# Identity products ahead of the first product, and a later release for the memory tokens' preparation

## The chip, the cores and the metric

The kernel runs on one core of one Trainium2 chip. The metric is the device time of one execution in microseconds (us), as the median of several runs. Engines are named as in the profile: PE is TensorE (matrix products), DVE is VectorE, ACT is ScalarE, POOL is GpSimd, SP is the engine that issues the DMAs.

## The reference

One decoder layer for 1024 tokens of width 1024 in float32: a normalisation, two groups of heads side by side (a gated recurrent one, the mLSTM, and a forgetting attention), a cross-attention into 256 memory tokens, a squared-ReLU MLP and a last normalisation. The part around the change is the start of it:

```python
xn  = rmsnorm(x, ln1)                    # x: 1 x 1024 x 1024
...                                      # w_in (1024 x IN_COLS) gives q, k, v, gates of both groups
b   = jnp.cumsum(fc, axis=-1)            # log forget gates, per head
m_t = jnp.maximum(b + m, jnp.max(dmat, axis=-1))
...
memn = rmsnorm(mem, ln_mem)              # 256 memory tokens, used much later
k, v = jnp.split(memn @ w_kv, 2, axis=-1)
```

## The kernel before

**Products.** A float32 product is made of three products in the chip's rounded format float32r: each operand is cut into a high part (a copy on ACT, L132 or L135) and a low part (a subtraction on DVE, L133 or L136), and `mm3` (L184, L185, L186) adds low times high, high times low and high times high in one PSUM bank. So a weight or an activation can be used only when both engines have cut it.

**The first stage (L372 to L407).** It computes the mLSTM values of the first two heads and the gates, for 8 tiles of 128 tokens, from x with 1024 input channels in 8 steps k. The first half of the tokens has its 4 tiles in the banks `mm`, `tp`, `m2` (printed as `m` in some views) and `tp`: for each k four tiles times three products, 12 products of 128x272. The second half has three tiles in the `sc` banks and, after the stage, the fourth in `mm`. Before a step k its weights (`cut_w`) and its x (`cut_x`) are cut. Sums of squares of x are added into `wide` on DVE (L361), and give the reciprocal root `rcol` (L196, L204 to L206, POOL between). `first_sink(hf, t)` then reads a bank on ACT and DVE, scales by `rcol`, and writes the values (L135, L136) and the gates' column (L370). The block `with in_order()` keeps PE, ACT, DVE and POOL in the written order; the rest of the program is ordered by a scheduler from costs of its own.

**What follows.** `token_major` makes the values of the other two heads, 8 tiles of 24 products (128x256), in the banks `tp`, `m2`, `tp`, `sc`, `mm`, `sc`, `sc` and so on in turn; each tile is read by ACT (L135) and DVE (L136). On the way stand the gates: DVE works out a polynomial of the gates (L427 to L431), PE transposes the result (L446, L451), ACT copies it (L447), DVE scans it twice along the tokens (L452, L456), and PE transposes again (L467). Then come projections with 128x512 products: `conv_silu` (tile `tp`, and a second half in `mm`) and `fx_project` (tile `m2`). Their weights are loaded (L172) into two buffers `wr` and cut by L132 and L133.

**The memory tokens.** `mem_prepare` (L280 to L294) works on `mem` in four chunks of 128x512. A chunk is loaded into a buffer `r_f` (L284; there are two), squared on ACT (L220, `r_c`), added up on DVE (L224, `r_b`, from the second chunk on), cut with the gain in two halves (ACT L135 into `r_p`, DVE L136 in place in `r_f`), and both parts are stored to `hmd` in DRAM (L292). A third load must wait until the first chunk's store has emptied its buffer. `hmd` is read back by one DMA at L1040.

The call stands far down in the code, under a release:

```python
banks[:] = ["mm", "tp", "m2", "tp"]
with tc.issue_after(last_sum.ins):
    mem_prepare()
ready = ml_project(0)
```

`issue_after(ins)` puts the block's instructions that run on the engine of `ins` behind `ins` in that engine's queue. `last_sum` is an addition on DVE, so this holds for the DVE instructions of `mem_prepare` (L224, L136); it is an order and not a wait, and the loads of the first two chunks need none of these instructions.

```python
    square_to(wide[2], 1, 7)
    add_to(wide[1], wide[0])
    last_sum = add_to(wide[1], wide[2])
tiles[1].append(ps_tile("mm")[:, :WV])
for k in range(KT):
    first_values(1, k, (3,))
rsqrt_sums(wide[1], rcol[:, 4:8], 4, 2)
for t in range(4):
    first_sink(1, t)
```

PSUM is dealt out by tag: three `sc` banks, two `tp`, and one each of `mm`, `m2` and `ov`. A tile that takes over a bank waits until its last tile was read.

## Time and profile before

| | us |
|---|---|
| median of 3 runs | 1536.44 |
| the three runs | 1536.03, 1536.44, 1536.86 |
| the profiled execution's own time | 1535.99 |
| its span | 1534.2 |
| PE busy | 1507.5 (98%) |
| DVE busy | 1111.3 (72%) |
| ACT busy | 731.0 (48%) |
| POOL busy | 508.5 (33%) |
| PE idle before its first product | 7.47 |

The span runs from the first to the last instruction that the profile records. A row of the timeline gives start, duration, engine, line, operation, output<-input, shape and count, and in brackets the idle time before it with what ended it. A row of the waits gives who waited for whom, the total, the number of times and the longest. The mean granted clock of PE over the span is 0.998 of full.

### The profile page before, as it was taken

The page shows a single profiled execution, that of the slowest core. Times are in us where ns is not written, and L with a number is a line of the kernel's source. Part 1 is how long each engine was busy: PE and PEld are TensorE (multiplying, and loading weights), DVE is VectorE, ACT ScalarE, POOL GpSimd, SP SyncE. Part 2 cuts the span into 40 slices and gives each one's busy share as a digit, 9 for nine tenths or more (in the row PEclk, how much of TensorE's full clock was granted, in tenths as well). Part 3 has the DMA queues.
Part 4 walks back from the last instruction along what each step waited for, and adds up shares of the span by engine and source line. Part 5 has one row for each costly group of instructions (what it writes and reads, how often), then busy time and mean ns, then how long its engine had stood idle before and what let it go on. Part 6 is the DMA issues. An engine that isn't in the chain of part 4 may idle for free. (4 is left out here: it accounts for less than half of the span.)

```text
span 1534.2 us, 22052 instructions
## 1 busy us (share of the span) xinstructions
PE 1507.5 (98%) x7729; PEld 1262.1 (82%) x7729; DVE 1111.3 (72%) x1716; ACT 731.0 (48%) x1365; POOL 508.5 (33%) x543
## 2 busy tenths in 40 slices
PE   8999999999999999999999999999999999999997
PEld 8878888889898887788888877787787888888887
DVE  7756666764788884854457889898887667887665
ACT  7324343434687773543444457665665621121224
POOL 0002130404355441521110023545455365663322
PEclk9999999999999999999999999999999999999999
DMA  6422233446787958963334528776667777676623
GB/s 215 131 79 76 96 104 112 129 138 161 238 250 217 290 195 280 315 206 125 124 125 164 172 93 299 240 254 240 230 243 273 303 285 283 268 272 237 245 96 110
DMA packets 121531, 303.54 MB, mean 198 GB/s; under 512 B 13502, under 2 KB 28152, under 8 KB 113996
## 3 DMA queue, kind: packets, MB, share of 16 engines
q1 hardware_dynamic: 121420, 302.13, 57.7%
q8 instruction: 61, 1.00, 0.3%
q14 instruction: 50, 0.41, 0.1%
HBM read 202.22 MB, written 99.86 MB: 197 GB/s over the span
## 5 line engine op out<-in xcount | busy, mean ns | idle before, releaser
L184 PE MATMUL tp<-act,wl 128*128 128x512 f32 (+1 forms) x448 | 176.4, 394 | 1.2 <-ACT row L1339 0.7
L185 PE MATMUL tp<-act,wh 128*128 128x512 f32 (+1 forms) x448 | 175.6, 392 | 0.0
L186 PE MATMUL tp<-act,wh 128*128 128x512 f32 (+1 forms) x448 | 175.1, 392 | 0.0
L133 DVE TENSOR_TENSOR wl<-wr,wh 128x1024 fp32r<-128x1024 f32 (+2 forms) x99 | 129.6, 1309 | 25.2 <-ACT wh L132 24.7
L132 ACT ACTIVATE wh<-wr 128x1024 fp32r<-128x1024 f32 (+2 forms) x99 | 99.1, 1001 | 88.8 <-PE tp L186 34.3
L184 PE MATMUL mm<-act,wl 128*128 128x512 f32 (+1 forms) x336 | 130.6, 389 | 1.4 <-DVE r_c L518 0.9
L186 PE MATMUL mm<-act,wh 128*128 128x512 f32 (+1 forms) x336 | 129.2, 384 | 0.0
L185 PE MATMUL mm<-act,wh 128*128 128x512 f32 (+1 forms) x336 | 128.9, 384 | 0.0
L184 PE MATMUL m<-act,wl 128*128 128x512 f32 (+1 forms) x312 | 120.7, 387 | 1.6 <-DVE r_a L916 1.3
L186 PE MATMUL m<-act,wh 128*128 128x512 f32 (+1 forms) x312 | 119.5, 383 | 0.0
L185 PE MATMUL m<-act,wh 128*128 128x512 f32 (+1 forms) x312 | 119.2, 382 | 0.0
L184 PEld LDWEIGHTS tp<-act,wl 128*128 128x128 f32 x448 | 84.3, 188 | 21.0 <-ACT row L1339 1.2
L186 PEld LDWEIGHTS tp<-act,wh 128*128 128x128 f32 x448 | 84.3, 188 | 19.1
L185 PEld LDWEIGHTS tp<-act,wh 128*128 128x128 f32 x448 | 84.4, 188 | 18.7
L184 PE MATMUL sc<-act,wl 128*128 128x512 f32 (+1 forms) x248 | 97.1, 392 | 0.9 <-DVE wl L133 0.8
L185 PE MATMUL sc<-act,wh 128*128 128x512 f32 (+1 forms) x248 | 96.8, 390 | 0.0
L186 PE MATMUL sc<-act,wh 128*128 128x512 f32 (+1 forms) x248 | 96.8, 390 | 0.0
L132 ACT ACTIVATE wh<-z 128x1024 fp32r<-128x1024 f32 (+1 forms) x54 | 55.5, 1028 | 82.6 <-POOL z L1410 59.8
L1410 POOL TENSOR_TENSOR z<-wr 128x256 f32<-128x256 f32 x56 | 50.5, 923 | 131.2 <-DMA wr<-w_ff2q 114.3
L133 DVE TENSOR_TENSOR wl<-z,wh 128x1024 fp32r<-128x1024 f32 (+1 forms) x54 | 74.5, 1380 | 8.1 <-ACT wh L132 7.9
L132 ACT ACTIVATE w<-wr 128x768 fp32r<-128x768 f32 (+2 forms) x31 | 25.5, 823 | 105.0 <-PE tp L184 32.5
L184 PEld LDWEIGHTS mm<-act,wl 128*128 128x128 f32 x336 | 63.4, 189 | 14.3 <-DVE r_c L518 1.2
(685 smaller groups left out, 4286.2 us busy)
## 6 DMA issues: line engine op xcount, KB each, us to landing
act<-right SPq DMA_DIRECT2D x49, 1024.0 KB
right<-w SPq DMA_DIRECT2D x56, 256.0 KB
wr<-w_ff2q SPq DMA_DIRECT2D x28, 512.0 KB
right<-r_d SPq DMA_DIRECT2D x49, 256.0 KB
right<-r_e SPq DMA_DIRECT2D x49, 256.0 KB
act<-fqk SPq DMA_DIRECT2D x48, 256.0 KB
wr<-w_in SPq DMA_DIRECT2D x20, 512.0 KB
wr<-w_ff SPq DMA_DIRECT2D x20, 512.0 KB
```

Source lines behind the costliest of these rows:

```text
L132: s.activation(hi, src, AF.Copy)
L133: return v.tensor_tensor(out=lo, in0=src, in1=hi.bitcast(F32), op=ALU.subtract)
L184: nc.tensor.matmul(ps, w[1], x[0], start=first, stop=False, skip_group_check=more)
L185: nc.tensor.matmul(ps, w[0], x[1], start=False, stop=False, skip_group_check=more)
L186: nc.tensor.matmul(ps, w[0], x[0], start=False, stop=last, skip_group_check=more)
L1410: g.tensor_tensor(out=o, in0=x, in1=y, op=op)
```

## The change

Two edits. Right after the constants, 28 matrix products of the 128x128 identity with itself are written into an `ov` bank that nothing reads, so they stand first in PE's queue. And the block of `mem_prepare` is released by the last instruction of the last `first_sink` of the first stage (L370, on DVE) in place of `last_sum` (L361, on DVE).

```diff
     vec = const("vec", [P, a["vec"].shape[1]])
 
+    busy = ov_()
+    for _ in range(28):
+        nc.tensor.matmul(busy[:, :P], ident, ident, start=True, stop=True)
+
     def split(hi, lo, src, scale=None):
...
         mv_sink(4 * hf + t, 0, ps[:, :256])
-        v.tensor_scalar(out=z[:, 4 * hf + t], in0=ps[:, 256:], scalar1=rcol[:, 4 * hf + t : 4 * hf + t + 1], scalar2=None, op0=ALU.mult)
+        return v.tensor_scalar(out=z[:, 4 * hf + t], in0=ps[:, 256:], scalar1=rcol[:, 4 * hf + t : 4 * hf + t + 1], scalar2=None, op0=ALU.mult)
...
         add_to(wide[1], wide[0])
-        last_sum = add_to(wide[1], wide[2])
+        add_to(wide[1], wide[2])
...
     for t in range(4):
-        first_sink(1, t)
+        last_sink = first_sink(1, t)
...
-    with tc.issue_after(last_sum.ins):
+    with tc.issue_after(last_sink.ins):
         mem_prepare()
```

Since the scheduler orders what is outside `in_order()`, the second edit also moves other instructions; all differences lie in the first 100 us. In the changed kernel every line from 129 on has a number 4 higher (L136 is L140, L446 is L450), and buffers count one or some more. The prediction uses the line numbers of before.

On DVE, around the second reciprocal root (`rcol`), before:

```order
L204 TENSOR_TENSOR c_t_37_439<-c_y_36_437 128x4
L205 SCALAR_TENSOR_TENSOR c_t_37_439<-c_t_37_439,c_var_35_435 128x4
L224 TENSOR_TENSOR r_b_64_776<-r_c_71_801,r_b_64_776 128x512
L206 SCALAR_TENSOR_TENSOR rcol_80<-c_t_37_439,c_y_36_437 128x4
L136 SCALAR_TENSOR_TENSOR r_f_70_799<-r_f_70_799,vec_77,r_p_72_804 128x256 x2
L136 SCALAR_TENSOR_TENSOR act_8_94<-m2_48_523,rcol_80,act_8_94 128x2x128
```

and after:

```order
L208 TENSOR_TENSOR c_t_38_468<-c_y_37_466 128x4
L209 SCALAR_TENSOR_TENSOR c_t_38_468<-c_t_38_468,c_var_36_464 128x4
L210 SCALAR_TENSOR_TENSOR rcol_109<-c_t_38_468,c_y_37_466 128x4
L140 SCALAR_TENSOR_TENSOR act_9_123<-m2_49_552,rcol_109,act_9_123 128x2x128
L140 SCALAR_TENSOR_TENSOR act_8_122<-sc_23_158,rcol_109,act_8_122 128x2x128
```

The sum and the cuts of the third chunk (`r_b`, `r_f`) have left this place; the read of the `m2` bank follows `rcol` directly.

On DVE, in the gates' polynomial (`w4`), ahead of the read of the sixth value tile of `token_major` (in the bank `tp_57_665` before, `tp_58_694` after) and the first scan, before:

```order
L430 SCALAR_TENSOR_TENSOR w4_28_135<-w4_28_135 128x96
L136 SCALAR_TENSOR_TENSOR act_8_94<-m2_56_638,rcol_80,act_8_94 128x2x128
L430 SCALAR_TENSOR_TENSOR w4_28_135<-w4_28_135 128x96 x5
L431 SCALAR_TENSOR_TENSOR w4_28_135<-w4_28_135 128x96
L136 SCALAR_TENSOR_TENSOR act_8_94<-tp_57_665,rcol_80,act_8_94 128x2x128
L452 SCALAR_TENSOR_TENSOR act_39_473<-w4_40_474,act_39_473 12x1024
```

and after:

```order
L140 SCALAR_TENSOR_TENSOR act_9_123<-m2_57_667,rcol_109,act_9_123 128x2x128
L434 SCALAR_TENSOR_TENSOR w4_29_164<-w4_29_164 128x96
L228 TENSOR_TENSOR r_b_65_805<-r_c_72_830,r_b_65_805 128x512
L434 SCALAR_TENSOR_TENSOR w4_29_164<-w4_29_164 128x96
L140 SCALAR_TENSOR_TENSOR r_f_71_828<-r_f_71_828,vec_77,r_p_73_833 128x256 x2
L434 SCALAR_TENSOR_TENSOR w4_29_164<-w4_29_164 128x96
L228 TENSOR_TENSOR r_b_65_805<-r_c_75_842,r_b_65_805 128x512
L140 SCALAR_TENSOR_TENSOR r_f_74_840<-r_f_74_840,vec_77,r_p_76_845 128x256
L434 SCALAR_TENSOR_TENSOR w4_29_164<-w4_29_164 128x96
L140 SCALAR_TENSOR_TENSOR r_f_74_840<-r_f_74_840,vec_77,r_p_76_845 128x256
L140 SCALAR_TENSOR_TENSOR act_9_123<-tp_58_694,rcol_109,act_9_123 128x2x128
```

The third and fourth chunk's sums and cuts now stand here, ahead of the read of the `tp` bank.

On PE, around the gates' transposes (from `w4`, L446 and L451), before:

```order
L446 MATMUL mm_52_609<-ident_65,w4_28_135 12x128 x4
L446 MATMUL sc_53_615<-ident_65,w4_28_135 12x128 x4
L451 MATMUL sc_54_621<-ident_65,w4_28_135 4x128 x4
...
L467 MATMUL ov_60_746<-ident_65,act_39_473 128x4 x8
L184 MATMUL tp_90_879<-act_5_91,wl_87_848 128x512
L185 MATMUL tp_90_879<-act_6_92,wh_86_847 128x512
L186 MATMUL tp_90_879<-act_5_91,wh_86_847 128x512
```

and after:

```order
L188 MATMUL tp_91_908<-act_6_120,wl_88_877 128x512
L189 MATMUL tp_91_908<-act_7_121,wh_87_876 128x512
L190 MATMUL tp_91_908<-act_6_120,wh_87_876 128x512
...
L450 MATMUL mm_53_638<-ident_65,w4_29_164 12x128 x4
L450 MATMUL sc_54_644<-ident_65,w4_29_164 12x128 x4
L455 MATMUL sc_55_650<-ident_65,w4_29_164 4x128 x4
...
L471 MATMUL ov_61_775<-ident_65,act_40_502 128x4 x8
L188 MATMUL tp_91_908<-act_6_120,wl_88_877 128x512
```

Seven of the eight groups of three of the `tp` projection (`conv_silu`) now stand ahead of the transposes; one is left behind L471, and the 24 of the `m2` projection (`fx_project`) follow it. The new tile `tp_91_908` takes over the bank of `tp_58_694`.

## The prediction

> **What bounds the kernel now.** I read first the busy line and the chain of the page, then TensorE's waits, then the timeline of the places the change touches.

> ```profile
> PE 1507.5 (98%) x7729; PEld 1262.1 (82%) x7729; DVE 1111.3 (72%) x1716; ACT 731.0 (48%) x1365; POOL 508.5 (33%) x543
> PE 34%; DVE 3%; issue 1%; ACT 1%; DMA 0%; DVEq 0%; POOLq 0%; POOL 0%; ACTq 0%
> ```

> TensorE (PE) is busy 98% of the span, and the chain runs mostly through it. So a microsecond is won only where PE idles or works slowly, and lost wherever PE is made to wait. Of its waits three lie near the edits:

> ```profile
> PE mm L184 <- DVE wl L133: 7.5, 1, 7.5
> PE m L184 <- DVE act L136: 0.8, 1, 0.8
> PE mm L184 <- DVE r_c L518: 0.9, 1, 0.9
> ```

> They are the idle start before the first product, a wait for a bank that VectorE (DVE) has not read, and one at 95 us. All numbers below are microseconds on the clock of the profiled run of before, whose own time is 1535.99.

> **Part 1: the identity products.**

> ```profile
> 1.24 0.29 POOL L118 TENSOR_SCALAR_AFFINE_SELECT ident<-ident 128x128 f32<-128x128 f32 x1
> 7.47 0.57 PE L184 MATMUL mm<-wh,act 128*128 128x272 f32 x1 [7.47 <-DVE wl L133]
> 10.33 0.43 PE L184 MATMUL mm<-wh,act 128*128 128x272 f32 x1
> 12.83 0.29 PE L184 MATMUL mm<-wh,act 128*128 128x272 f32 x1
> 14.31 0.29 PE L184 MATMUL mm<-wh,act 128*128 128x272 f32 x1
> 21.83 0.29 PE L184 MATMUL sc<-wh,act 128*128 128x272 f32 x1
> 14.91 0.75 DVE L136 SCALAR_TENSOR_TENSOR act<-act,vec,act 128x512 fp32r<-128x512 f32 x1
> 1504.61 1.05 PE L211 MATMUL mm<-ident,c_r 128*128 128x128 f32 x8
> ```

> The `mm` rows are the first of the 12 products of each k. The first two groups take 10.33−7.47=2.86 and 12.83−10.33=2.50, the third 14.31−12.83=1.48: early products run at half rate. Full rate would save 12.83−7.47−2×1.50=2.36. The identity is ready at 1.24+0.29=1.53. Eight products of its shape take 1.05, so 0.13 each, at most doubled while slow: 28 take under 28×0.26=7.3 and about 28×0.21=5.9 by the ratio of the slow and fast groups. They end near 7.5, inside TensorE's idle time before 7.47, on an engine that has nothing else to do; nothing waits for the bank they write. At the worst end they finish at 8.8, and then eight fast groups of 1.50 would end at 20.8 instead of the value below.

> How much of the 2.36 arrives? With groups of 1.50 from 7.47 the sixth (k=5) would start at 14.97, but its operand's low part is done only at 14.91+0.75=15.66. From there three groups end at 15.66+3×1.50=20.16, where before the next stage starts at 21.83. The gain is 1.65, with 0.67 of spare time ahead of k=5; the ends are 2.36 (if the cut of k=5 moves up too) and 1.0 (products late as above: 21.83−20.8). Everything up to the last product of this stage and the next follows PE, so I carry the 1.65 on as a shift. [...]

> **Part 2a: the bank wait that goes.**

> ```profile
> 46.26 0.28 PE L186 MATMUL tp<-wh,act 128*128 128x256 f32 x1
> 47.37 0.38 PE L184 MATMUL m<-wh,act 128*128 128x256 f32 x1 [0.83 <-DVE act L136]
> 44.70 0.63 ACT L220 ACTIVATE r_c<-r_f 128x512 f32<-128x512 f32 x1 [1.74 <-DMA r_f<-mem]
> 43.75 0.16 DVE L205 SCALAR_TENSOR_TENSOR c_t<-c_t,c_var 128x4 f32<-128x4 f32 x1
> 45.36 0.69 DVE L224 TENSOR_TENSOR r_b<-r_c,r_b 128x512 f32<-128x512 f32 x1 [1.46 <-ACT r_c L220]
> 45.97 0.15 DVE L206 SCALAR_TENSOR_TENSOR rcol<-c_t,c_y 128x4 f32<-128x4 f32 x1
> 46.05 0.87 DVE L136 SCALAR_TENSOR_TENSOR r_f<-r_f,vec,r_p 128x256 fp32r<-128x256 f32 x2
> 46.84 0.48 DVE L136 SCALAR_TENSOR_TENSOR act<-m,rcol,act 128x256 fp32r<-128x256 f32 x1
> ```

> PE's next slot was 46.38; it started at 47.37: 0.99 lost. DVE's read of the bank (46.84) stood behind L224, which waited for a memory load. In the changed order L206 follows L205 directly (43.75+0.20−1.65=42.3), and the read is done by 43.1, against a slot at 46.38−1.65=44.73. Gain 0.99. PE is then 1.65+0.99=2.64 ahead.

> **Part 2b: the tp bank.** The memory pieces now stand later on DVE, two of them (the third and fourth chunk, each one load, one square, two cuts and two stores) among the L430s, ahead of the read of the sixth token tile's tp bank. PE in turn has 21 of the 24 products of the next projection (tp, 128x512) ahead of the gate transposes L446, and their first needs that bank.

> ```profile
> 49.22 0.23 DVE L370 TENSOR_SCALAR w<-mm,rcol 128x16 f32<-128x16 f32 x1
> 54.00 0.25 DVE L430 SCALAR_TENSOR_TENSOR w<-w 128x96 f32<-128x96 f32 x1
> 54.16 0.48 DVE L136 SCALAR_TENSOR_TENSOR act<-m,rcol,act 128x256 fp32r<-128x256 f32 x1
> 38.25 1.72 SPq L292 DMA_DIRECT2D hmd<-r_f  x2
> 40.68 0.33 SPq L284 DMA_DIRECT2D r_f<-mem  x1
> 53.82 0.25 ACT L248 ACTIVATE row<-ov 8x128 f32<-8x128 f32 x1
> 56.50 0.60 PE L446 MATMUL mm<-ident,w 128*12 128x128 f32 x4
> 45.24 0.89 ACT L135 ACTIVATE r_p<-r_f,vec 128x256 fp32r<-128x256 f32 x2
> 56.70 0.47 ACT L135 ACTIVATE act<-tp,rcol 128x256 fp32r<-128x256 f32 x1 [2.64 <-PE tp L186]
> 387.76 0.46 SPq L1040 DMA_DIRECT2D act<-hmd  x1
> 57.21 0.48 DVE L136 SCALAR_TENSOR_TENSOR act<-tp,rcol,act 128x256 fp32r<-128x256 f32 x1 [0.94 <-ACT act L135]
> ```

> PE is free for them where L446 stood: 56.50−2.64=53.86. If the third memory load is there in time, ScalarE (ACT) squares it (L220) behind the L248 copy: 53.82+0.25−2.64=51.4, plus 0.63 is 52.0. From there DVE has two L224 (45.97−45.36=0.6 each), four L136 of r_f (46.84−46.05=0.8 for two) and three L430 (54.16−54.00=0.16 each), 3.3 in all, then the read of the bank, 0.48: 55.7. PE loses 55.7−53.86=1.8.

> If the load is late: the last first_sink (L370) ends 49.22+0.23−46.84=2.6 after the read that ends part 2a begins, 45.2. Chunk 0's cut, the first memory work behind it, takes 0.88; its store to hmd goes out at about 46.15, the next load 2.43 after it (38.25 to 40.68), at 48.6. A load took up to 44.70−40.68=4.02: 52.6, L220 to 53.25, and 3.8 later 57.05, a loss of 3.2. The fourth load waits for chunk 1, which DVE leaves 0.6+0.8 after chunk 0, at 47.5; by the same steps it lands by 54.1, is squared by 54.7, and with one L224, two cuts, one L430 and the read behind it (2.0) gives 56.8 at most, inside these ends. ACT's part of this read (56.70) stands behind the same chunks' squares and two cuts each (0.89) there, so it ends at 54.7+0.89+0.47=56.1 at the latest, and DVE's part, which must follow it, at 56.6: also inside. On SP the third weight load now goes ahead of the first store and the row's two transfers ahead of the last four stores; the memory is read back only at 387.76, so I cost this at nothing, and POOL's order is unchanged. Without memory work in the way the bound is 57.21+0.48−56.50=1.2. I take the middle of 1.8 and 3.2: **2.5**.

> **Part 2c: the gate chain.** The transposes L446 start a chain over ACT and DVE, two scans (L452, L456), behind which DVE cuts the weights (L133 at 65.53) of the projection that follows (`m`, 128x512).

> ```profile
> 58.23 2.28 DVE L452 TENSOR_TENSOR_SCAN act<-w,act 12x1024 f32<-12x1024 f32 x1 [0.54 <-ACT act L447]
> 65.53 1.20 DVE L133 TENSOR_TENSOR wl<-wr,wh 128x1024 fp32r<-128x1024 f32 x1
> 64.15 0.50 PE L184 MATMUL tp<-act,wl 128*128 128x512 f32 x1
> 69.85 0.39 PE L184 MATMUL m<-act,wl 128*128 128x512 f32 x1
> ```

> From L446 to those weights: 65.53+1.20−56.50=10.2. Before, PE filled this with 64.15−56.50=7.65 of products and 24 of the projection in 69.85−64.15=5.70, so it came to `m` at 69.85, 3.1 after they were ready at 66.73. Now 21 of the 24 are spent ahead of L446; three remain, 0.71, and 7.65+0.71=8.36. PE waits 10.23−8.36=**1.87**. The order is fixed on both engines; the bounds are 0 (the chain speeds up by as much) and 2.6 (its scans wait once more).

> **Sum.** −1.65−0.99+2.5+1.87=+1.7; with 1.8 to 3.2 for part 2b, +1.0 to +2.4. The wait at 95 us (L518, 0.9) keeps its length, since both sides move together. Own time 1535.99+1.7=1537.7; the median of the runs is 1536.44, 0.45 above the profiled run: **1538.1**, with 1537.4 to 1538.9 as the case's own range. This is under 0.2% (3.07 us), about what a measurement of this kernel can tell from no change; so faster is under 1533.4 and slower over 1539.5.

> **Rivals.**

> *A. The new waits don't come.* DVE may find both memory chunks loaded and pass them while PE is still in the sc products, and the weights may be cut ahead of the second scan. Then −2.64: 1533.8, or 1532.9 if the L518 wait goes too. For it: L224 had only one wait of this kind in before (1.46). Against it: DVE is one queue, the read stands behind all of these pieces in it, and 3.3 of them are plain work that no early load removes; and the gate chain is 10.2 long whatever the loads do. If only one comes, −2.64+1.87 or −2.64+2.5: 1535.7 to 1536.3.

> *B. The identity products raise no clock.* Then 1.65 is missing: 1539.8. No row shows the clock after identity products alone. [...]

> *C. The new waits cost the clock as well: slower.* The kernel's end shows what a stall can do:

> ```profile
> 1527.30 0.71 PE L211 MATMUL mm<-ident,c_r 128*128 128x128 f32 x4 [1.62 <-DVE c_r L1552]
> 1525.00:1530.00 5.00, 1.39 (x10) 1.11 (x10) 2.54 (x9) 0.33 (x1) 0.71 (x1) 0.80 0.26 88
> ```

> (The second row is a window: its length, the busy times of PE, weight load, DVE, ACT and POOL, then granted clock, DMA share and GB/s.) In 1525 to 1530 PE is busy 1.39 of 5 and the mean granted clock 0.80, so about 2 of the 5 at half. A wait of 1.62 stands in it. The wait of part 2b (up to 3.2) could bring the same, and the restart cost 2.36 at the kernel's start: 1538.1+2.4=1540.5. [...] Against it: the 7.65 and 5.70 of dense work around it.

> **How the numbers follow.** The forecast 55% (1537.4 to 1538.9), one wait only 14% (1535.7 to 1536.3), A 9% (1533.8; half of that below 1533.4), B 8% (1539.8, half above 1539.5), C 14% (1540.5). Range 1535.0 to 1540.5: it holds the forecast, the single wait, B and half of C, 84%, and leaves out A and C's upper half, about 16%. Faster: half of A, 0.05. Slower: C and half of B, 0.18. Same: 0.77.

> **What would show it.** Right: the stage after the eight k-groups starts at about 20.2 and the fourth `mm` group is as short as the first; no wait of PE for act L136 at 45; one of 1.8 to 3.2 near 54 ahead of the 128x512 tp products; one near 1.9 for wl ahead of `m`. The part 2b term is wrong if r_f<-mem lands before 51.4 and DVE is through by 54; part 2c is wrong if `m` starts without idle time. Products at half rate behind either wait mean C; a slow first group after the identity products means B.

## The result, and the profile after

The changed kernel took 1546.14 us in the median (1544.14 to 1546.69), against 1536.44: ratio 1.0056, 95% interval 1.0044 to 1.0068. In a second job it took 1543.60 against 1535.95: 1.0050 (1.0036 to 1.0064). So it is slower by 7.7 to 9.7 us where 1.7 was forecast. The profiled execution took 1544.14 with a span of 1542.4, 8.2 over the span of before; its page:

```profile
span 1542.4 us, 22160 instructions
PE 1516.6 (98%) x7785; PEld 1268.5 (82%) x7785; DVE 1112.8 (72%) x1716; ACT 731.2 (47%) x1365; POOL 507.1 (33%) x543
```

PE has 56 instructions more, not 28, and is busy 9 us longer. The timeline of PE after, at the places that the prediction spoke of:

```profile
1.58 7.86 PE L131 MATMUL ov<-ident 128*128 128x128 f32 x56 [1.58 <-POOL ident L118]
9.20 0.37 PE L188 MATMUL mm<-wh,act 128*128 128x272 f32 x1
21.32 0.29 PE L188 MATMUL sc<-wh,act 128*128 128x272 f32 x1
56.74 0.50 PE L188 MATMUL tp<-act,wl 128*128 128x512 f32 x1 [1.67 <-DVE act L140]
61.73 0.60 PE L450 MATMUL mm<-ident,w 128*12 128x128 f32 x4
72.02 0.50 PE L188 MATMUL m<-act,wl 128*128 128x512 f32 x1 [1.69 <-DVE wl L137]
72.92 0.63 PE L188 MATMUL m<-act,wl 128*128 128x512 f32 x1
76.47 0.39 PE L188 MATMUL m<-act,wl 128*128 128x512 f32 x1
99.39 0.50 PE L188 MATMUL mm<-act,wl 128*128 128x512 f32 x1 [0.94 <-DVE r_c L522]
```

The identity products hold up the first product to 9.20. The `sc` row, the start of the next stage, stood at 21.83 and is 0.51 earlier. Both new waits are there, 1.67 and 1.69. Behind the second, products have 0.63 instead of 0.39. The last row stood at 95.56 in the kernel before, so PE is 3.83 late there:

```profile
95.56 0.50 PE L184 MATMUL mm<-act,wl 128*128 128x512 f32 x1 [0.94 <-DVE r_c L518]
```

The windows of the same trace (columns as in the prediction) show what the 0.63 is, and a second such place:

```profile
69.28:72.70 3.42, 1.73 (x9) 1.15 (x9) 3.42 (x4) 1.94 (x4) 0.00 (x0) 1.00 0.12 18
72.70:76.12 3.42, 3.42 (x10) 2.64 (x9) 3.42 (x6) 0.00 (x0) 0.00 (x0) 0.50 0.62 172
468.65:472.06 3.41, 0.84 (x6) 0.41 (x4) 0.07 (x1) 1.22 (x3) 0.51 (x1) 1.00 0.72 274
472.06:475.48 3.42, 3.01 (x11) 2.83 (x12) 3.01 (x8) 2.45 (x9) 0.78 (x1) 0.50 0.28 86
```

Each time a stretch of 3.4 us in which PE was about half busy or less (1.73, 0.84) is followed by one of 3.42 at a granted clock of 0.50. The second place is a wait that the kernel before has too, in the cross-attention, for a weight load; it has grown. Before, then after:

```profile
460.61 0.37 SPq L934 DMA_DIRECT2D wr<-w_xv  x1
464.88 0.63 ACT L946 ACTIVATE wh<-wr 128x512 fp32r<-128x512 f32 x1 [3.32 <-DMA wr<-w_xv]
466.51 0.50 PE L721 MATMUL sc<-act 128*128 128x512 f32 x1 [1.06 <-ACT act L734]
```

```profile
465.04 1.14 SPq L938 DMA_DIRECT2D wr<-w_xv  x1
470.84 0.63 ACT L950 ACTIVATE wh<-wr 128x512 fp32r<-128x512 f32 x1 [5.24 <-DMA wr<-w_xv]
472.47 0.80 PE L725 MATMUL sc<-act 128*128 128x512 f32 x1 [2.98 <-ACT act L738]
```

From issue to use the load takes 5.80 instead of 4.27, and PE waits 2.98 instead of 1.06. Laying PE's rows of the two traces side by side, row for row counted from the end, gives how far PE is ahead of or behind the kernel before. The changed kernel is 0.51 ahead after the first stage, 1.60 ahead at 54, 3.83 behind at 99, 4.05 behind at 464, 7.12 behind at 470, and 7.6 behind at 1500.

### The profile page after: what moved, and what is told of

It reads as the page before. It is cut to its first block, busy times and chain, and to the rows that moved or that the text cites. A ratio compares the mean times of both kernels' runs of the same rounds, so it can differ in the third digit from the quotient of the medians.

```text
span 1542.4 us, 22160 instructions
## 1 busy us (share of the span) xinstructions
PE 1516.6 (98%) x7785; PEld 1268.5 (82%) x7785; DVE 1112.8 (72%) x1716; ACT 731.2 (47%) x1365; POOL 507.1 (33%) x543
## 5 line engine op out<-in xcount | busy, mean ns | idle before, releaser
L136 ACT ACTIVATE wh<-wr 128x1024 fp32r<-128x1024 f32 (+2 forms) x99 | 99.0, 1000 | 94.2 <-PE tp L190 37.9
L136 ACT ACTIVATE wh<-z 128x1024 fp32r<-128x1024 f32 (+1 forms) x54 | 55.5, 1028 | 83.6 <-POOL z L1414 61.6
L136 ACT ACTIVATE w<-wr 128x768 fp32r<-128x768 f32 (+2 forms) x31 | 25.5, 824 | 104.1 <-PE tp L188 32.8
```

The source lines that it names most:

```text
L136: s.activation(hi, src, AF.Copy)
```

## The experiments

The question was first what of the 8.2 us is fixed and what is chance, and which part of the change brings it.

**The changed kernel once more** (no edit), for a second trace.

> The changed kernel once more, for a second profile. In the first profile the whole loss of 8.15 us of span was: first stage only 0.51 early, 1.67 and 1.69 of new waits, the clock at half from 72.70 to 76.12, and at 466 to 475 us a wait of 2.98 for a weight load (1.06 before) with the clock at half from 472.06 to 475.48. Theory 1 (the clock's windows lie free of the program): the two waits of 1.7 stay within 0.1, the first stage is 0.5 early again, but the places of the half-clock stretches differ, and the time is 1541 to 1547. Theory 2 (the loss at 466 is fixed, caused by the 4 us by which all is later): the wait of 3.0 at 472 and both half-clock stretches come again at the same places.

It took 1543.60 (1541.93 to 1544.80). Both waits came again (1.76 and 1.69); the first stage was 0.17 late this time. The wait for the load at 466 did not grow (0.9), but one at 604, for the residual's load and store, did. PE's timeline:

```profile
57.51 0.50 PE L188 MATMUL tp<-act,wl 128*128 128x512 f32 x1 [1.76 <-DVE act L140]
72.79 0.50 PE L188 MATMUL m<-act,wl 128*128 128x512 f32 x1 [1.69 <-DVE wl L137]
606.08 0.47 PE L188 MATMUL m<-act,wl 128*128 128x512 f32 x1 [2.11 <-DVE r_a L920]
```

and four windows of it, laid in whole steps of 3.413 us from 606.63, where its clock falls (the third from last column is the clock):

```profile
70.78:74.19 3.41, 1.72 (x8) 1.17 (x7) 3.41 (x5) 1.20 (x3) 0.00 (x0) 1.00 0.21 35
74.19:77.60 3.41, 3.41 (x17) 2.73 (x16) 3.41 (x5) 0.00 (x0) 0.00 (x0) 1.00 0.48 153
603.20:606.60 3.40, 1.29 (x6) 0.77 (x5) 2.11 (x4) 0.83 (x2) 1.26 (x2) 1.00 0.92 305
606.63:610.05 3.42, 3.42 (x10) 2.64 (x9) 0.30 (x1) 0.00 (x0) 0.00 (x0) 0.50 1.03 383
```

The same wait of 1.69 at 71 that cost half a window of clock in the first trace cost none here, and another wait did. Theory 1 holds so far: the two waits belong to the program, and the half-clock windows came elsewhere. Why 1.69 cost the clock once and not the other time is not shown: in both traces the whole wait lies inside one such window (69.28:72.70 and 70.78:74.19), with the same 1.69 of idle PE in it.

**The two parts apart.** `ident28` and `ident18` have the identity products alone, `sink` the later release alone.

```diff
# ident28: the change without the later release; ident18: the same with range(18)
-        add_to(wide[1], wide[2])
+        last_sum = add_to(wide[1], wide[2])
-    with tc.issue_after(last_sink.ins):
+    with tc.issue_after(last_sum.ins):
# sink: the change without the identity products
-    for _ in range(28):
-        nc.tensor.matmul(busy[:, :P], ident, ident, start=True, stop=True)
```

> The 28 identity products alone; the memory tokens' preparation is released as before. My theory (the identity products are 56 instructions of 0.11 to 0.21 us, and hold up the first real product): first product at 9.2, the stage after the eight groups at 21.3, 0.5 early, the wait of 0.8 for act at 46 stays, no wait at 55 and 70: 1535.4 to 1536.6 (from 1536.44). Rival (the identity products themselves are what made it slow, for example by the later phase of the program): above 1540.

> 18 identity products (36 instructions) alone, release as before. They would end at 1.58+13 x 0.213+23 x 0.111=6.9, ahead of the operands at 7.47. Theory: first product at 7.5 at full clock, next stage at 20.2, 1.65 early, and so 1534.3 to 1535.3. Rival (the gain is lost again at the wait for act at 46, whose reader waits for a load that does not move): 1535.8 to 1536.6.

> The later release alone, without identity products. Theory (the loss is of the moved order): the wait of 0.8 for act at 47 is gone, two waits of 1.5 to 2 at about 55 and 70 appear, with one half-clock stretch of 3.4 us (1.7 lost) or two: 1539.5 to 1545. Rival (the two parts only cost together): 1535 to 1537.

Medians beside 1535.95 of before on the same chip: `ident28` 1539.98 (ratio 1.0029, 1.0017 to 1.0042), `ident18` 1535.12 (0.9996, 0.9987 to 1.0005), `sink` 1541.02 (1.0036, 1.0023 to 1.0049). The parts add up: 4.0+5.1=9.1. In `sink`, PE waits 1.9 and 2.2 at the two places and one half-clock window follows at 72; PE is 3.9 behind at 99 us, and 5.0 at the end. So most of the release's share is the two waits and the clock. The rest comes late here too, with a second half-clock window behind a wait for the residual:

```profile
604.60:608.01 3.41, 1.47 (x7) 0.93 (x6) 1.69 (x3) 0.83 (x2) 0.86 (x1) 1.00 0.92 308
608.01:611.42 3.41, 3.41 (x10) 2.63 (x9) 0.00 (x0) 0.00 (x0) 0.00 (x0) 0.50 1.02 398
```

In `ident18` the first product stands at 7.83 and the next stage starts 1.1 earlier:

```profile
1.59 6.49 PE L131 MATMUL ov<-ident 128*128 128x128 f32 x36 [1.59 <-POOL ident L118]
7.83 0.37 PE L188 MATMUL mm<-wh,act 128*128 128x272 f32 x1
20.71 0.29 PE L188 MATMUL sc<-wh,act 128*128 128x272 f32 x1
```

The median gains 0.8 of it, within the scatter of both. `ident28` is the riddle: neither expectation (1535.4 to 1536.6, or above 1540 by the products themselves) says why its first trace, 1535.33, and its other runs, 1538.5 to 1543.4, differ.

**Is it POOL, or the time?** `dve28` multiplies a tile that DVE fills with ones; `ident46` has 46 products.

```diff
# dve28, in ident28
+    warm = w2("a", P)
+    v.memset(warm, 1.0)
-        nc.tensor.matmul(busy[:, :P], ident, ident, start=True, stop=True)
+        nc.tensor.matmul(busy[:, :P], warm, warm, start=True, stop=True)
```

> 28 products of a tile that DVE fills with ones (in place of the identity that POOL makes), otherwise as 28 identity products alone. Theory A (the spread and the 4 us of 28 identity products come from when POOL has the identity ready, which the profile shows at 1.5): without POOL 1535 to 1536.5. Theory B (it is the products): 1539 to 1541 as with the identity.

> 46 identity products alone (92 instructions), release as before. 28 of them alone gave a median of 1539.98 (1535.33 to 1543.35), 18 gave 1535.12. Theory A (their price is the time by which they hold up the first real product, at 0.213 cold until about 5 us and 0.111 after that): they end near 13.4, the first stage ends 3.6 later than before, 1539 to 1541 and hardly more than 28 cost. Theory B (outside the profiled execution they run at the cold 0.213 throughout: 28 end at 13.5, 46 at 21.2): 1546 to 1549.

`dve28` took 1538.42 (1536.80 to 1542.01; ratio 1.0019, 1.0010 to 1.0028), between the two expected ranges and nearer to that of theory B. `ident46` took 1542.04 (1.0042, 1.0027 to 1.0058), 1 above the range of theory A and 4 below that of theory B. So POOL is not needed for the loss, and half rate throughout is not the cause either. With 46 products the first product starts at 14.09 and PE is 5.07 behind from 50 us on, of 6.1 in the median: nearly all of its loss is early. With 28, it is not.

**More traces of 28 identity products alone, and of before.**

> 28 identity products alone, a second trace. The first trace had 1535.33, five further executions 1538.5 to 1543.4. Theory 1 (the price is chance later in the program: loads that land late at about 466 and 605 and the half-clock window that follows a wait of 1.5 and more): up to 380 us the shift against before lies between -0.5 and +1.4, and the rest, 3 to 6, is in one or two jumps at 466 and 600 to 650, each with a wait of PE of over 1.5. Theory 2 (the identity products end later than in the first trace): the first product starts after 12 and the shift of 3 to 5 is there from the first stage on.

> 28 identity products alone, a third trace; as for the second.

> 28 identity products alone, a fourth trace; as for the second.

> The kernel before, a second trace. Theory 1: the clock rises at another time than 12.52 (8 to 14), the jumps at 466 and 600 to 650 against the first trace are below 1.5 and so draw no half-clock window: 1534.5 to 1537. Rival (the late loads and half-clock windows are as frequent here): over 1537 with a stretch at half clock.

They took 1541.10, 1542.66 and 1537.98; before 1536.95. From 50 to 380 us the four traces of `ident28` lie between -0.08 and +0.22 of before: the first stage's gain and loss cancel. Nearly everything else comes at 466 and from 600 to 660: at 1500 us they are -0.6, 4.8, 6.7 and 1.5 behind. The second trace of before loses 2.1 between 610 and 665 us as well, so a late value of one trace is uncertain by about that. PE's wait for the residual at 600 in the timeline of before, then in that of `ident28_b`, and the window behind it there:

```profile
602.47 0.47 PE L184 MATMUL m<-act,wl 128*128 128x512 f32 x1 [1.26 <-DVE r_a L916]
```

```profile
603.28 0.76 PE L188 MATMUL m<-act,wl 128*128 128x512 f32 x1 [2.42 <-DVE r_a L920]
```

```profile
603.00:606.30 3.30, 3.02 (x7) 2.47 (x8) 1.13 (x3) 0.00 (x0) 0.00 (x0) 0.50 0.96 324
```

All four traces with 28 products have a half-clock window there or at 658; the two of before have none until the end. That fits theory 1, which put the loss at these places. Its waits "of 1.5 and more" were my estimate from those that a half-clock window had followed until then (1.62 at 1527 in before, 1.69 and 2.98 in the changed kernel); waits of 1.6 and 1.5 between 590 and 670 in the second trace of before brought none. But it looks like more than chance: with 28 the loads land late in four traces of four.

**Number or time?** Two theories are left for the late loss: C, that it goes by the number of PE instructions ahead, and D, that it goes by the time that they take. `mix28` has as many PE instructions ahead as 28 products but the time of some 18, `wide18` the reverse; `pad28` adds 18 tiny products to the 28.

```diff
# mix28, in ident28
-    for _ in range(28):
+    for _ in range(12):
         nc.tensor.matmul(busy[:, :P], ident, ident, start=True, stop=True)
+    for _ in range(16):
+        nc.tensor.matmul(busy[:4, :4], ident[:, :4], ident[:, :4], start=True, stop=True)
# wide18, in ident28: wide_ is 128x208, all ones
-    for _ in range(28):
-        nc.tensor.matmul(busy[:, :P], ident, ident, start=True, stop=True)
+    for _ in range(18):
+        nc.tensor.matmul(busy[:, :208], ident, wide_, start=True, stop=True)
# pad28, in ident28, and after_pad, in the changed kernel: behind the 28
+    for _ in range(18):
+        nc.tensor.matmul(busy[:4, :4], ident[:, :4], ident[:, :4], start=True, stop=True)
```

> 12 identity products of 128x128 and 16 of 4x4 ahead of the first product, release as before: as many PE instructions as 28 identity products of 128x128 (56 products and 56 weight loads), but about the time of 18. Theory C (what costs 3 to 5 us late in the program with 28 is the number of instructions, which moves the places where PE's program is fetched, 256 instructions at a time, against the loads at 466 and 590 to 660): 1538 to 1541. Theory D (it is the time at which the first stage ends): 1534.5 to 1536, as with 18.

> 18 products of the identity with a tile of ones, 208 columns wide, release as before: as many instructions as 18 identity products, but about the time of 28 (36 x 0.17). Theory C (number of instructions): 1535 to 1537. Theory D (time): 1538 to 1541.

> 28 identity products and 18 more of 4x4 behind them, release as before: 184 added PE instructions, as many as 46 identity products have, where 28 alone add 112. The 18 small ones take 36 x 0.03=1.1 more. Theory C (the late loss goes by the number of instructions ahead, and 184 is a good number: 46 products lost about 1 late): 1536.5 to 1538.5, faster than 28 alone (1540) although there is more to do. Theory D (time): 1541 or more.

> The changed kernel with the same 18 small products added behind its 28. Theory C: 1541 to 1543, under the changed kernel's 1543.6 to 1546.1. Theory D: 1545 to 1547.

In the table, each product row counts with its weight load, so 28 products are 112 instructions. "Early" is how far PE is behind before at 380 us (negative: ahead), from each kernel's trace (for `ident28`, of all four); "late" is the median's difference from before on the same chip, less "early".

| kernel | PE instructions added | early | median against before | late |
|---|---|---|---|---|
| sink | 0 | 3.9 | 5.1 | 1.1 |
| ident18 | 72 | -0.9 | -0.8 | 0.1 |
| wide18 | 72 | 2.1 | 1.5 | -0.6 |
| ident46 | 184 | 5.1 | 6.1 | 1.0 |
| pad28 | 184 | 0.9 | 1.6 | 0.7 |
| after_pad | 184 | 6.5 | 6.4 | -0.1 |
| ident28 | 112 | 0.0 | 4.0 | 4.0 |
| dve28 | 112 | -0.3 | 2.5 | 2.8 |
| mix28 | 112 | -1.9 | 1.1 | 3.0 |
| changed kernel, first job | 112 | 3.8 | 9.7 | 5.9 |
| changed kernel, second job | 112 | 3.1 | 7.7 | 4.6 |

(`mix28` 1537.06 and `wide18` 1537.44 beside 1535.98, ratios 1.0009, 1.0000 to 1.0017, and 1.0013, 1.0004 to 1.0021; `pad28` 1538.10 beside 1536.55, 1.0013, 1.0004 to 1.0022.) The expected times for `mix28` and `wide18` were missed by both theories, because their early parts were mis-guessed; by the last column theory C (number) fits and theory D (time) does not: the kernels with 112 instructions lose 2.8 to 5.9 late, those with 0, 72 or 184 lose -0.6 to 1.1. The changed kernel and `sink` are equally late at 380 us (3.8 and 3.9), and lose 5.9 and 1.1 behind it. `pad28` and `after_pad` (1542.98 beside 1536.55, ratio 1.0038, 1.0025 to 1.0050) do more than the kernels that they add to, and lose less, both as theory C expected. An early value comes from one trace, in which a half-clock window more or less is 1.7, and is set against a median; the two groups lie 1.7 apart at their nearest (2.8 and 1.1).

The traces alone say much the same. Of the ten with 112 added instructions (the later `after_hi` and `neg28` among them) nine have a half-clock window between 466 and 661 us; of the other ten, both of before included, one has (`sink`, shown above). Counted inside each trace from 380 us to the end of the span, the ten lose -0.6 to 7.3, 3.5 on average, and the other nine -0.9 to 1.1 against the first trace of before.

Why the number matters stays open. The page counts 61 instruction packets of 16 KB on the queue q8 (1.00 MB), one to 255 of the changed kernel's 15570 products and weight loads. So I take them to be PE's program, which no row of the profile says; added instructions move the times of these packets against the other loads. In the traces the last one ahead of the wait at 602 us starts 20 to 21 us before it with 112 added, 26 with 184 and 11 with 72 (each trace's lateness at 600 us taken off). So they move with the number, but none lies at the wait, and that they are the cause is not shown.

**Taking the second wait away.** `after_hi` is the changed kernel with the products of the `m` projection's first half in another order, those that need no low part of the weights first (excerpt).

```diff
+            if high and not half:
+                for k in range(kn):
+                    hi = wv[0][:, k, n * P : (n + 1) * P]
+                    nc.tensor.matmul(ps, hi, x[half][1][:, k], start=k == 0, stop=False)
+                    nc.tensor.matmul(ps, hi, x[half][0][:, k], start=False, stop=False)
+                for k in range(kn):
+                    nc.tensor.matmul(ps, wv[1][:, k, n * P : (n + 1) * P], x[half][0][:, k], start=False, stop=k == kn - 1)
+                ...
```

> The changed kernel, but in the first half of the first fx_project the 16 products with the weights' high part stand ahead of the 8 with the low part (16 x 0.233=3.7 us of work for a wait of 1.7). Theory (the wait for the low part and the clock that it takes with it cost 1.7 to 3.4): no wait at 70 to 72, no half-clock stretch at 72, 1540 to 1543. Rival (the wait only moves, since the scans set the pace of all that follows): 1543.5 to 1546.5 as the changed kernel.

1542.00 (1539.88 to 1544.49), ratio 1.0036 (1.0023 to 1.0050). Its waits of PE from 40 to 110 us:

```profile
PE tp L188 <- DVE act L140: 1.7, 1, 1.7
PE mm L188 <- DVE r_c L531: 0.9, 1, 0.9
```

The wait for `wl` is gone and no half-clock window follows; at 99 us PE is 0.37 behind before instead of 3.83. The wait and its clock window are thus worth 3.5. Against before on each chip, 1.6 to 3.7 of it show in the median, which still carries the late loss: this trace has half-clock windows at 469 and 609.

**Other numbers and another release.** `after18` is the changed kernel with 18 products; `neg18` and `neg28` release the memory tokens' work by the negation at the end of the gates' chain (L464 after), with 18 and 28.

```diff
# neg18, neg28
-        v.tensor_scalar(out=neg[0:MLH], ...)
+        gate_end.append(v.tensor_scalar(out=neg[0:MLH], ...))
-    with tc.issue_after(last_sink.ins):
+    with tc.issue_after(gate_end[0].ins):
```

> The changed kernel with 18 identity products in place of 28. The later release alone cost 5.1 (1541.0), 18 products alone gave 0.8, 28 alone cost 4.0, both 7.7 to 9.7. If the parts add up: 1540 to 1541.5, 3 to 5 under the changed kernel, with the two waits at 55 and 70 still there. Rival (the identity products cost through the two waits, by bringing PE there earlier): 1543 and more.

> 18 identity products, and the memory tokens' preparation released by the last instruction of the gates' chain on DVE (the negation behind the second scan). PE's order around the gates is then that of before. Theory: 1.65 and 0.99 gained, no wait at 55 or 70: 1533.0 to 1534.6. Rival (the memory pieces, now behind the scans, delay the chain to L518): a wait of 2 to 3 at 95, 1535 to 1537.

> As the version with 18 identity products and the release behind the gates' chain (1534.54), but with 28. Theory C and D both: 1537.5 to 1540 (28 alone cost 4.8 more than 18 alone). Rival (28 costs only the 0.9 by which the first stage ends later): 1535 to 1536.

`after18` 1540.14 beside 1535.98 (1.0029, 1.0017 to 1.0040): the parts add up here too, with waits of 2.1 and 1.9. PE is 3.7 behind at 380 us, and only 0.5 of the median comes later. `neg18` 1534.54 beside 1535.95 (0.9987, 0.9978 to 0.9996) is faster than both kernels: PE's order around the gates is that of before, there is no wait at 47, 55 or 70, and PE is 2.2 ahead from 50 to 70 us. Its trace then loses 2.8: at 79 PE waits 0.99 for the memory tokens' sums, and a half-clock window follows at 81. That trace is the slowest of the kernel's runs (1536.09). `neg28` 1539.51 (1.0024, 1.0013 to 1.0035): 28 instead of 18 costs 5.0 once more, though both stand within 1.1 of each other at 300 us. By the table's count the late part is -2.0 for `neg18`, whose early part holds that half-clock window, and 4.0 for `neg28`.

## Why the prediction was wrong

- **Part 1, the price of the products: mis-sized.** Eight rows of L211 were taken for eight products. Each float32 product of the identity left two rows here: 28 products are 56 rows (18 are 36), 0.21 each until 4.44 and 0.11 behind. They end at 9.4, beyond the 8.8 given as the worst, and the gain is 0.51, not 1.65. With 18 products it was 1.1. The clock does rise on identity products (from 4.44 on, and from 5.89 on in the second trace, both ahead of the first product at 9.20 and 9.89; before had slow rows to 12.4), so rival B is out.
- **Part 2a: right.** The read of the `m2` bank goes ahead, 0.99 forecast, 1.09 measured.
- **Part 2b: right, at its early end.** The square of the third chunk (L224 after, L220 before) started straight behind the copy to `row`, at 52.25, so the load was there. PE was free at 56.50-1.60=54.90 and started at 56.74, a loss of 1.84 (1.8 to 3.2 forecast, 2.5 taken).

```profile
52.10 0.25 ACT L252 ACTIVATE row<-ov 8x128 f32<-8x128 f32 x1
52.25 0.61 ACT L224 ACTIVATE r_c<-r_f 128x512 f32<-128x512 f32 x1
```

- **Part 2c: right.** From L450 at 61.73 PE needs 8.36 to `m`, so 70.09; it started at 72.02: 1.93, forecast 1.87.
- **Rival C: it happened, at a lower price.** I priced it at 2.4 and gave it 14%. Half the clock followed a wait of 1.69 in the first trace (not in the second), about as long as the 1.62 at the kernel's end, and cost 3.42 at half clock, 1.7. Together: -0.51-1.09+1.84+1.93+1.71=3.88, and the trace shows 3.83 at 99 us.
- **The sum that stops at 95 us: the step that failed.** I wrote that the wait there "keeps its length, since both sides move together", and put everything behind it at nothing, so that it would move as one. The two traces of the changed kernel lose another 3.8 and 3.2 between 380 and 1500 us, most of it at 466 in the first and at 600 to 610 in the second. There PE waits for loads (2.98 and 2.11), and a half-clock window follows each wait. The profile of before has these waits too (1.06 at 466, 1.26 at 602); the prediction names neither. No rival held a loss far from the change. Why these loads come later in the program's time with the 28 products is open; the runs show only that it goes with the number of instructions added.
- **How much each part weighs.** At 99 us the trace is 3.83 late where the sum had 1.7. With nothing lost behind it, the prediction's own way from the profiled run to the median (0.45 more) would give 1535.99+3.83+0.45=1540.3, just inside the stated range. The late loss carries the result out of it.

## What to carry to other kernels

Count instructions by rows of the same data type: here 28 products of one line were 56 rows. A wait of PE of 1.69 us cost another 1.7 at half clock in one trace of two, and the waits of 1.06 at 466 and 1.26 at 602 in the kernel before grew to 2.98 and 2.11 behind a change in the first 100 us, so list the waits of the whole program before saying that the rest moves as one. When a prefix is padded, try several lengths, since 18 products came out level with before, or 1.4 us ahead with the release of `neg18`, and 28 lost 2.5 to 4.0.
